# A 3x3 convolution with 2x2 max pooling: rows 33 to 63 of the first image pair in one casting load, the second pair's first 33 rows in another, and a new order

## Chip, cores and metric

The kernel runs on one core of one Trainium2 chip. The metric is the device time of one execution in microseconds (us). The engines are TensorE (PE, with its weight loads as PEld), VectorE (DVE), ScalarE (ACT), GpSimd (POOL) and SyncE (SP, which here only issues transfers). Each has its own instruction queue and works through it in order; semaphores hold an instruction back until what it needs is done.

## The reference

```python
x:      16 images, 64 channels, 64 x 64, float32
weight: 128 x 64 x 3 x 3, float32
conv[b, co] += weight[co, ci, kh, kw] * x_pad[b, ci, kh:kh+64, kw:kw+64]      # padding 1
output[b, c, i, j] = max(conv[b, c, 2i:2i+2, 2j:2j+2])                        # 16 x 128 x 32 x 32
```

## The kernel before

**Tiles.** Two images make a pair: the 64 channels of the first lie on partitions 0 to 63, those of the second on 64 to 127. There are 8 pairs, each in SBUF as one bf16 tile `xb[p]` of 66 rows (a zero row above and below). A pair is cut in four quarters of 16 image rows, which give 8 pooled rows; a quarter of one image (half `h` = 0 or 1) has 8 x 64 = 512 columns, one PSUM bank of `acc`. The 32 quarters are numbered `s` in the order of work; `PLACES` says which pair and quarter of it `s` is (0, 1, 3, 5 are the first pair, 2, 4, 6, 7 the second, 8, 9, 10, 11 and so on the next ones). The last quarter, 31, is done in two halves, 31 and 32.

**Arithmetic.** For a pooled row one needs the larger of two convolution rows, even and odd. What both have in common is added once, after the maximum. Quarters of type K form two accumulators from raw rows, `ta` = (G2-G1) x[2i+1] + G0 x[2i-1] and `tb` = (G0-G1) x[2i] + G2 x[2i+2], and add G1 (x[2i] + x[2i+1]) to the larger. Quarters of type W (27 of 32) use differences: e = x[2i] - x[2i+1], d = x[j+1] - x[j-1], s = x[2i] + x[2i+1]; `ta` = GM e + G0 d, `tb` = GM e + G2 d, and GP s is added to the larger of -`ta` and `tb`. GM and GP are half of G0 + G2 minus or plus G1. Every product is three matmuls, one for each column tap, on 64 partitions; those of the two halves run side by side on the two halves of PE's rows.

**Order.** The whole program is the text `ORDER`. Each word is one step, taken in this order and put on its engine's queue, so the text fixes every queue. A word is a name, the quarter and the half; `+` chooses the other engine (or way), `&` does two things in one instruction. The names that matter here:

- `g0a`, `g0b`, `g1`, `g2` cast weight blocks on ACT; `D0`, `D2a`, `D2b`, `GS`, `GM`, `GP` form their differences and sums on DVE (`GS` with `+`); `u..` copies a block's first slot behind its last (a ring copy); `T..` and `H..` transpose a block on PE; `V..` copies it out of PSUM.
- `L.p.lo.hi` is a load of rows lo to hi of pair p by POOL, cast from float32 to bf16 on the way (line 325). `XOa`, `XOb`, `XEa`, `XEb` and `X1` to `X4` are casts on ACT or DVE of rows that SP has loaded as float32 (lines 430 and 432).
- `F.k.part` are the products of quarter 0. `PA1`, `PA2`, `PB1`, `PB2`, `PR` are those of type K, `P2` (e), `P0` and `P3` (d), `P1` (s) those of type W. A product waits in a list until the other half has one too, then the six matmuls are issued in turn. The first product of an accumulator takes the next bank from `BANKS`, and PE then waits until whatever held that bank has been read.
- `D`, `E`, `S` form d, e, s (lines 319 and 304). For d the plain word is POOL and `+` is DVE; for e `+` is POOL; s is always on DVE. `Da` and `Db` are the two halves of a d.
- `SE` copies `ta` to a bank for `tb` after P2 (ACT, line 352); `EV` copies `ta` to SBUF (line 346, or 342 for type K); `MX` takes the maximum on DVE (line 380); `OD` copies the odd columns on ACT (line 390); `CM` takes the maximum over columns on DVE (line 409). With `OD+` there is no copy and `CM` reduces both columns itself (line 405). When both halves are done, the result is stored from SP (line 422).

An instruction on POOL is made to wait for the last SBUF operation on DVE that stands before it in `ORDER`:

```python
def on_vector(inst):
    sbuf_op[0] = inst
    return inst

def on_gpsimd(inst):
    behind(inst, sbuf_op[0])
    return inst
```

The first pair's rows 0 to 48 come as float32 through SP (`kfirst` in two parts, `ksecond`, `kthird`) and are cast on ACT and DVE; rows 49 to 63 and all other pairs come through POOL's casting loads.

Of the kernel before, what the change touches and what calls it, by code (L numbers as in the profile page):

```python
# [11 lines left out]
def kernel(  # L12
# [85 lines left out]
    kthird = const.tile([128, 2 * R, W], FP32)  # L98
    nc.sync.dma_start(out=kthird, in_=rows_of(0, FAR + 2 * R, FAR + 4 * R))
# [206 lines left out]
    def row_sum(s, alt, joint):  # L306
        combine("s", s_pool, ADD, s, joint, False)
# [145 lines left out]
    for m in PRODUCTS:  # L453
        steps[m] = lambda s, h, m=m: product(m, s, h)
    either = {
        "GS": outer_sum, "D": lambda s, alt: row_d(s, not alt, 0, 2 * span_of(s)[1]),
        "Da": lambda s, alt: row_d(s, alt, 0, R),
        "Db": lambda s, alt: row_d(s, alt, R, 2 * R),
         "SE": seed, "EV": evac, "OD": odd,
# [12 lines left out]
    for m in ("G1", "G2"):  # L472
# [14 lines left out]
        OD.0.1 P0.3.1 P3.3.1 PA2.5.0 EV.3.1 P0.3.0 MX.1.0 CM.0.1 PA1.5.1 PR.1.0 EV.3.0 D+.2 MX.3.1 E&.2
        PB1.5.0 PR.1.1 EV.5.0 OD.1.1 OD.1.0 S&.4 P1.3.1 P2.2.1 P3.3.0 CM.1.1 CM.1.0 D.4 OD.3.1 CM.3.1 SE.2.1
        PB2.5.0 MX.3.0 P2.4.0 PA2.5.1 P2.4.1 MX.5.0 EV.5.1 P0.2.1 E&.6 P1.3.0 P3.2.1 SE.4.0 SE.4.1 OD.3.0 D+.7
        CM.3.0 P0.4.1 PR.5.0 EV.2.1 OD.5.0 P0.4.0 EV.4.1 P2.6.0 D+.6 P3.4.1 MX.2.1 SE.6.0 E+.8 P2.6.1 MX.4.1  # L490
        P1.2.1 P3.4.0 P0.6.0 P3.6.0 CM.5.0 P1.4.1 EV.4.0 S&.6 SE.6.1 EV.6.0 S&.10 OD.2.1 CM.2.1 P0.6.1 PA1.9.0
        P2.7.0 EV.6.1 OD.4.1 PA2.9.0 P3.6.1 MX.4.0 D.10 P1.4.0 PB1.5.1 PB2.5.1 L.4.0.64 MX.6.1 P1.6.1 SE.7.0
        P2.8.1 EV.9.0 MX.6.0 MX.5.1 OD.4.0 PR.5.1 P0.7.0 EV.7.0 D+.8 CM.4.0 P1.6.0 OD.6.1 SE.8.1 CM.6.1 P0.8.1
        P2.7.1 P3.7.0 OD.6.0 CM.4.1 CM.6.0 OD.5.1 E&+.10 P2.8.0 SE.8.0 EV.8.1 P3.8.1 PB1.9.0 CM.5.1 P0.8.0
        P2.10.1 MX.7.0 SE.7.1 PB2.9.0 EV.8.0 P3.8.0 SE.10.1 S&.13 P0.7.1 EV.7.1 P1.7.0 Db.13 S&.9 MX.9.0
        PR.9.0 P2.2.0 P3.7.1 OD.7.0 MX&.8.1 P0.10.1 P3.10.1 P1.8.1 P1.8.0 D.11 CM.7.0 E&+.12 EV.10.1 MX.7.1
        SE.2.0 P1.7.1 MX.10.1 OD.9.0 CM.9.0 OD.8.0 CM.8.0 OD.8.1 CM.8.1 P1.10.1 P2.11.0 PA1.15.1 OD.7.1 CM.7.1
        SE.11.0 P0.2.0 P3.2.0 PB1.9.1 EV.2.0 OD.10.1 S&.14 PA2.15.1 P2.10.0 P0.11.0 MX.2.0 P1.2.0 PB2.9.1
        L.5.0.64 CM.10.1 SE.10.0 EV.15.1 PA1.9.1 E.19 OD.2.0 P0.10.0 EV.11.0 EV.10.0 P3.10.0 P2.11.1 PA2.9.1
        Da.13 S&.18 SE.11.1 E&.17 P3.11.0 CM.2.0 P2.12.1 PA1.15.0 EV.9.1 MX.10.0 P1.10.0 MX.11.0 MX.9.1  # L500
        P0.11.1 D.12 D+.16 SE.12.1 OD.10.0 CM.10.0 EV.11.1 PA2.15.0 P3.11.1 MX.11.1 E+.14 PR.9.1 P0.12.1
# [25 lines left out]
        E+.30 P1.27.1 OD+.27.1 Db+.28 P2.30.1 P1.27.0 EV.29.0 MX.29.0 SE.30.1 P2.28.0 P0.28.1 P3.28.1 CM.27.1
        OD.27.0 CM.27.0 D.30 P1.29.0 P2.30.0 S.30 EV.28.1 P0.30.1 MX.28.1 SE.28.0 OD.29.0 CM.29.0 EV.30.1 D.31
        E+.31 P2.29.1 P0.28.0 SE+.30.0 SE.29.1 P3.30.1 P3.28.0 P0.30.0 P1.28.1 EV.28.0 MX.30.1 P3.30.0 P0.29.1
        P2.31.1 MX.28.0 OD.28.1 CM.28.1 EV.30.0 MX.30.0 P3.29.1 SE.31.1 P1.28.0 P2.31.0 P1.30.0 P0.31.1 S.31  # L530
        EV.29.1 OD.28.0 SE.31.0 MX.29.1 P0.31.0 PA1.32.0 PA2.32.0 CM.28.0 EV.31.1 PB1.32.0 PRA.32.0 P1.30.1
# [68 lines left out]
```

## Time and profile before

| | us |
|---|---|
| three runs | 102.54, 102.1, 101.49 |
| median | 102.1 |
| profiled run | 101.6 |
| its span | 99.7 |
| first product on PE | 6.54 |
| end of the last matmul | 95.46 |
| last stores issued | 96.36 (SP), 96.56 (ACT) |

Times inside a run are counted from the start of the span. The granted clock is 1.00 in every stage up to the last matmul. Until about 28 us the DMA engines are busy all the time, with the casting loads from 7.5 on:

| load | issued | landed |
|---|---|---|
| weights, SP | 0.74 | 3.7 |
| `kfirst`, two parts | 1.17, 1.64 | 4.6, 5.9 |
| `ksecond` (512 KB of float32) | 2.11 | 7.6 |
| `kthird` (512 KB of float32) | 2.58 | 8.9 |
| L.0.49.64 (240 KB of bf16) | 6.28 | 10.9 |
| L.1.0.17 (272 KB) | 6.97 | 13.5 |
| L.1.17.33 (256 KB) | 7.50 | 14.7 |
| L.1.33.64 (496 KB) | 8.58 | 17.3 |
| L.2.0.33 (528 KB) | 9.10 | 20.1 |
| L.2.33.64 (496 KB) | 12.23 | 23.0 |
| L.3.0.64 (1024 KB) | 14.02 | 28.2 |

In the lines of the profile, "L193 PE" is line 193 of the kernel on PE; `out<-in` are the tiles; in lists by group the figures after the bar are busy time and the mean in ns of one instruction, then the idle time before them and what ended it; in a timeline the first two figures are start and duration, x the number of instructions merged, and the bracket the idle time before.

### The profile page before, as it was taken

The page shows a single profiled execution, that of the slowest core. Times are in us where ns is not written, and L with a number is a line of the kernel's source. Part 1 is how long each engine was busy: PE and PEld are TensorE (multiplying, and loading weights), DVE is VectorE, ACT ScalarE, POOL GpSimd, SP SyncE. Part 2 cuts the span into 40 slices and gives each one's busy share as a digit, 9 for nine tenths or more (in the row PEclk, how much of TensorE's full clock was granted, in tenths as well). Part 3 has the DMA queues.
Part 4 walks back from the last instruction along what each step waited for, and adds up shares of the span by engine and source line. Part 5 has one row for each costly group of instructions (what it writes and reads, how often), then busy time and mean ns, then how long its engine had stood idle before and what let it go on. Part 6 is the DMA issues. An engine that isn't in the chain of part 4 may idle for free.

```text
span 99.7 us, 2469 instructions
## 1 busy us (share of the span) xinstructions
PE 94.7 (95%) x887; PEld 58.2 (58%) x887; DVE 91.7 (92%) x196; ACT 84.5 (85%) x190; POOL 54.4 (55%) x45
## 2 busy tenths in 40 slices
PE   6999999999999999999999999999999999999920
PEld 2478445546647777855556566666665555556910
DVE  2498999999999999999999999999999999999960
ACT  5498797998899898999989999999999998999610
POOL 2047031733783951748397966963946499690000
PEclk9999999999999999999999999999999999999995
DMA  2999999999999889999079995999253060630363
GB/s 33 347 349 129 149 217 211 222 238 227 262 215 198 191 301 177 207 188 362 28 105 214 202 315 78 197 167 371 65 196 107 7 210 0 210 108 0 117 207 102
DMA packets 11036, 18.03 MB, mean 181 GB/s; under 512 B 784, under 2 KB 9104, under 8 KB 10384
## 3 DMA queue, kind: packets, MB, share of 16 engines
q0 software_dynamic: 1584, 7.59, 42.8%
q1 hardware_dynamic: 9296, 10.16, 30.0%
q8 instruction: 7, 0.11, 0.5%
q10 hardware_dynamic: 144, 0.13, 0.4%
q14 instruction: 5, 0.04, 0.1%
HBM read 17.07 MB, written 8.39 MB: 255 GB/s over the span
## 4 chain that ended last, share of the span: by engine, by line
PE 94%; DVE 1%; DVEq 0%; issue 0%
PE acc L193 89%; PE acc L544 4%; PE acc L145 2%; DVE o L398 1%; DVEq L595 0%
## 5 line engine op out<-in xcount | busy, mean ns | idle before, releaser
L193 PEld LDWEIGHTS <-wt 64*128 64x128 bf16 x858 | 55.5, 94 | 32.8 <-issue 3.8
L193 PE MATMUL acc<-d,wt 64*128 64x512 bf16 (+3 forms) x324 | 66.6, 373 | 0.0
L193 PE MATMUL acc<-s,wt 64*128 64x504 bf16 (+3 forms) x204 | 45.5, 367 | 0.0
L319 POOL TENSOR_TENSOR d<-xb 128x1024 bf16<-128x1024 bf16 (+1 forms) x18 | 33.3, 1860 | 18.3 <-DVE s L304 9.8
L380 DVE TENSOR_TENSOR acc<-acc,ev 128x512 f32<-128x512 f32 (+1 forms) x60 | 40.0, 685 | 1.1 <-PE acc L193 0.3
L193 PE MATMUL acc<-e,wt 64*128 64x512 bf16 (+2 forms) x162 | 40.1, 373 | 0.0
L346 ACT ACTIVATE ev<-acc 128x512 f32<-128x512 f32 (+1 forms) x54 | 31.9, 597 | 2.5 <-PE acc L193 2.0
L352 ACT COPY acc<-acc 128x512 f32<-128x512 f32 (+1 forms) x53 | 30.4, 576 | 3.0 <-PE acc L193 0.9
L193 PE MATMUL acc<-xb,wt 64*128 64x512 bf16 (+7 forms) x168 | 24.6, 327 | 0.0
L390 ACT COPY od<-acc 128x256 f32<-128x256 f32 (+1 forms) x54 | 19.0, 375 | 2.2 <-PE acc L193 1.8
L409 DVE TENSOR_TENSOR o<-acc,od 128x256 f32<-128x256 f32 (+1 forms) x54 | 20.7, 412 | 0.1
L304 POOL TENSOR_TENSOR e<-xb 128x512 bf16<-128x512 bf16 (+1 forms) x9 | 14.2, 1583 | 3.7 <-DVE d L319 3.7
L325 POOL DMA_DIRECT2D xb<-in_x_dram x11 | 6.2, 562 | 12.8 <-DVE wt L159 5.0
L304 DVE TENSOR_TENSOR s<-xb 128x1024 bf16<-128x1024 bf16 (+1 forms) x18 | 11.5, 646 | 0.2 <-ACT xb L430 0.2
L319 DVE TENSOR_TENSOR d<-xb 128x1024 bf16<-128x1024 bf16 (+1 forms) x12 | 7.8, 649 | 0.0
L405 DVE TENSOR_REDUCE o<-acc 128x256 f32<-128x512 f32 x10 | 6.8, 681 | 0.0
L342 ACT COPY ev<-acc 128x512 f32<-128x512 f32 x9 | 5.2, 592 | 0.7 <-PE acc L193 0.7
L304 DVE TENSOR_TENSOR e<-xb 128x1024 bf16<-128x1024 bf16 (+1 forms) x8 | 5.0, 619 | 0.0
L544 PE MATMUL acc<-const-bfloat16-1.0 128*128 128x512 bf16 x8 | 3.6, 626 | 0.8 <-PEq L581 0.8
L170 ACT CAST wq<-wraw 128x192 bf16<-128x192 f32 (+2 forms) x4 | 1.7, 444 | 1.7 <-DMA wraw<-in_weight_dram 1.7
L145 PEld LDWEIGHTS <-wq 128*128 128x128 bf16 x21 | 1.7, 117 | 1.7 <-DVE wq L443 0.9
L443 DVE TENSOR_TENSOR wq<-wraw 128x192 bf16<-128x192 f32 x1 | 0.5, 499 | 2.2 <-DMA wraw<-in_weight_dram 2.2
(27 smaller groups left out, 21.6 us busy)
## 6 DMA issues: line engine op xcount, KB each, us to landing
out_dram<-o SPq DMA_DIRECT2D x31, 256.0 KB, 4.3
xb<-in_x_dram POOLq DMA_DIRECT2D x5, 1024.0 KB, 9.6
xb<-in_x_dram POOLq DMA_DIRECT2D x2, 496.0 KB, 9.7
xb<-in_x_dram POOLq DMA_DIRECT2D x1, 528.0 KB, 11.0
ksecond<-in_x_dram SPq DMA_DIRECT2D x1, 512.0 KB, 5.5
kthird<-in_x_dram SPq DMA_DIRECT2D x1, 512.0 KB, 6.3
wraw<-in_weight_dram SPq DMA_DIRECT2D x1, 288.0 KB, 3.0
kfirst<-in_x_dram SPq DMA_DIRECT2D x1, 288.0 KB, 3.5
```

Source lines behind the costliest of these rows:

```text
L193: nc.tensor.matmul(acc[:, t, i0:i1, o0:o1], wt[lo : lo + CI, tap_of(m0, kw, h), :], rows(lo, i0, i1, c0, c1), start=start and kw == 1, sto ...
L304: note(engine.tensor_tensor(out=dst, in0=in0, in1=in1, op=op))
L319: engine.tensor_tensor(out=diffs[s][:, lo:hi, :], in0=t[:, f + 1 + lo : f + 1 + hi, :], in1=t[:, f - 1 + lo : f - 1 + hi, :], op=SUB)
L325: inst = on_gpsimd(nc.gpsimd.dma_start(out=xb[p][:, lo + 1 : hi + 1, :], in_=rows_of(p, lo, hi)))
L342: (nc.vector.tensor_copy if alt else nc.scalar.copy)(out=dst, in_=src)
L346: nc.scalar.mul(dst, src, -1.0)
L352: (nc.vector.tensor_copy if alt else nc.scalar.copy)(out=acc[:, t, i0:i1], in_=acc[:, ta[s, h], i0:i1])
L380: nc.vector.tensor_tensor(out=t, in0=t, in1=ev[s][:, h, i0:i1], op=MAX)
L390: nc.scalar.copy(out=dst, in_=acc[:, tb[s, h], i0:i1, 1::2])
L405: nc.vector.tensor_reduce(out=o[:, h, i0:i1], in_=t.rearrange("p r (w two) -> p r w two", two=2), axis=mybir.AxisListType.X, op=MAX)
L409: nc.vector.tensor_tensor(out=o[:, h, i0:i1], in0=t[:, :, 0::2], in1=od[s][:, h, i0:i1], op=MAX)
L544: nc.tensor.matmul(acc[:, n].rearrange("p a b -> p (a b)"), ones[:, 0:128], ones, start=True, stop=True, skip_group_check=True)
```

## The change

1. `kthird` and its transfer go, with the casts `X3` and `X4` (both on ACT). The casting load of rows 49 to 63 becomes one of rows 33 to 63. Quarter 3 (rows 32 to 47) now gets its rows from it.
2. L.1.0.17 and L.1.17.33 become L.1.0.33. L.2.33.64 comes ahead of L.2.0.33, L.7 ahead of L.6.
3. `GM` and `GP` may run on either engine (`outer`), and `GP` runs on POOL. s may run on POOL: it does so for five words of `ORDER` (quarter 15 alone, and in one instruction for the pairs of quarters at 21, 23, 24 and 31).
4. The results of quarters 12, 16 and 20 are stored in two transfers, one for each image, instead of one.
5. `ORDER` and `BANKS` are new from the first word to the last. PE has the same instructions, 858 product matmuls and 21 transposes among them. 17 transposes stand before the first product (20 before), and four, TGP, HGM and HGP, behind PA1 of quarter 1. Among the choices of engine: VG0 and VG2 go from DVE to ACT, XEa from ACT to DVE, X1 from DVE to ACT; 13 d of full size are on DVE (10 before); 12 odd copies are left out (10 before).

```diff
     ksecond = const.tile([128, 2 * R, W], FP32)
     nc.sync.dma_start(out=ksecond, in_=rows_of(0, FAR, FAR + 2 * R))
-    kthird = const.tile([128, 2 * R, W], FP32)
-    nc.sync.dma_start(out=kthird, in_=rows_of(0, FAR + 2 * R, FAR + 4 * R))
...
+    def outer(m, op, alt):
+        engine, note = (nc.gpsimd, on_gpsimd) if alt else (nc.vector, on_vector)
+        note(engine.tensor_tensor(out=slots(m), in0=gsum, in1=g1, op=op))
...
     def row_sum(s, alt, joint):
-        combine("s", s_pool, ADD, s, joint, False)
+        combine("s", s_pool, ADD, s, joint, alt)
...
+    SINGLY = (12, 16, 20)
...
-        if s < N - 1:
+        if s < N - 1 and s not in SINGLY:
             dst = out[2 * p : 2 * p + 2, :, q * R : (q + 1) * R, :].rearrange("b c h w -> c b (h w)")
             queue.dma_start(out=dst, in_=o.rearrange("p b h w -> p b (h w)"))
         else:
-            dst = out[2 * p + h, :, q * R : (q + 1) * R, :].rearrange("c h w -> c (h w)")
-            queue.dma_start(out=dst, in_=o[:, h].rearrange("p h w -> p (h w)"))
+            for k in (0, 1) if s < N - 1 else (h,):
+                dst = out[2 * p + k, :, q * R : (q + 1) * R, :].rearrange("c h w -> c (h w)")
+                queue.dma_start(out=dst, in_=o[:, k].rearrange("p h w -> p (h w)"))
...
-        "X3": lambda alt: cast_next(kthird, FAR + 2 * R, 0, alt),
-        "X4": lambda alt: cast_next(kthird, FAR + 2 * R, 1, alt),
...
     ORDER = """
-        D0 TD0 g1 D2a TG1 TD2 g2 TG2 uG1+ uD2+ HG1 GS+ D2b HD2 GM uG2+ uD0+ HG2 GP HD0 g0a VD2 L.0.49.64 TGM
-        VD0 L.1.0.17 uGM+ TG0 HGM VG1 TGP uG0+ g0b HG0 VG0+ L.1.17.33 XOa+ VG2+ XEa+ uGP F.0.0 XOb+ XEb+ S.0
-        VGM F.2.0 F.1.0 X1+ F.0.1 F.1.1 EV.0.0 F.2.1 F.3.0 F.3.1 PA1.1.0 X2 PB1.1.0 L.1.33.64 PA1.1.1 PB1.1.1
-        L.2.0.33 HGP PA2.1.1 X4 PB2.1.1 X3 VGP+ EV+.0.1 MX.0.0 PR.0.0 OD.0.0 PA2.1.0 MX.0.1 S.1 EV.1.1 E.3
...
+        g1 g0b uG1+ D0 TD0 D2a TG1 D2b GS+ L.0.33.64 uD0+ uD2+ HD0 TD2 HD2 g0a g2 TG0 uG0+ uG2+ VD2 TG2 GM XEa
+        HG0 XOa+ HG2 VG0 HG1 TGM F.0.0 VD0 F.2.0 XOb+ F.1.1 F.1.0 F.0.1 L.1.0.33 XEb+ F.2.1 VG2 F.3.0 F.3.1 X1
+        PA1.1.1 PA1.1.0 EV+.0.1 VG1 L.1.33.64 GP+ L.2.33.64 uGP EV.0.0 S.0 MX.0.1 uGM+ TGP X2 HGM HGP S.1
+        PB1.1.0 PR.0.1 PA2.1.0 OD.0.1 MX.0.0 PR.0.0 PB2.1.0 PA2.1.1 PB1.1.1 VGM Db.3 E.3 EV.1.0 OD.0.0 P2.3.1
+        S&.3 CM.0.1 P2.3.0 PB2.1.1 CM.0.0 PA1.5.1 VGP+ EV.1.1 Da+.3 PA1.5.0 SE.3.1 MX.1.0 PR.1.0 SE.3.0 P0.3.1
+        PA2.5.0 MX.1.1 PR.1.1 P0.3.0 EV.3.1 OD.1.0 L.2.0.33 D+.2 E&.4 P3.3.1 EV.5.0 S&.4 EV.3.0 P2.2.1 OD.1.1
+        CM.1.0 P3.3.0 SE.2.1 PA2.5.1 PB1.5.0 PB2.5.0 MX.3.1 MX.3.0 P1.3.1 P1.3.0 EV.5.1 OD.3.1 P2.4.1 CM.1.1
+        MX.5.0 P2.4.0 CM.3.1 L.3.0.64 D.4 E&.7 P0.2.1 OD.3.0 CM.3.0 SE.4.1 SE.4.0 PR.5.0 P3.2.1 P3.4.1 P0.4.1
...
+        EV.25.0 P0.26.0 CM.23.1 MX.25.0 SE.26.1 EV.26.0 CM.24.0 D.27 E+.30 E+.28 P3.26.0 P1.25.0 P2.27.1
+        MX.26.0 OD.25.1 SE.27.1 P2.27.0 P0.26.1 P3.26.1 P1.26.0 CM.25.1 E.29 P2.29.0 P0.27.1 D+.29 EV.26.1
+        OD.25.0 CM.25.0 P3.27.1 MX.26.1 SE.27.0 P2.28.1 P0.27.0 P3.27.0 P1.26.1 EV.27.1 MX.27.1 OD.26.0
+        CM.26.0 SE.29.0 EV.27.0 MX.27.0 SE.28.1 P1.27.1 P0.29.0 OD+.27.1 P3.29.0 P2.30.1 CM.27.1 EV.29.0
+        MX.29.0 OD.26.1 D.28 P0.28.1 D.30 E+.31 S&+.31 SE.30.1 P1.27.0 EV.28.1 P3.28.1 P2.28.0 CM.26.1
+        OD+.27.0 D.31 SE.28.0 CM.27.0 P0.30.1 P1.29.0 P2.29.1 P2.30.0 OD.29.0 EV.30.1 MX.28.1 P0.28.0 CM.29.0
...
```

More of the change, by code (lines that the diff above doesn't have):

```diff
@@ L455 @@
     either = {
-        "GS": outer_sum, "D": lambda s, alt: row_d(s, not alt, 0, 2 * span_of(s)[1]),
+        "GS": outer_sum, "GM": lambda alt: outer(GM, SUB, alt), "GP": lambda alt: outer(GP, ADD, alt),
+        "D": lambda s, alt: row_d(s, not alt, 0, 2 * span_of(s)[1]),
         "Da": lambda s, alt: row_d(s, alt, 0, R),
         "Db": lambda s, alt: row_d(s, alt, R, 2 * R),
-         "SE": seed, "EV": evac, "OD": odd,
+        "SE": seed, "EV": evac, "OD": odd,
         "XOa": lambda alt: cast_first(1, MID, alt),
@@ L487 @@
[L487 to L501, printed above, removed]
@@ L527 @@
[L527 to L531, printed above, removed]
@@ new lines @@
+        D+.6 OD.5.0 CM.5.0 D+.7 EV.2.1 MX.2.1 P2.6.1 P2.6.0 P1.2.1 P0.4.0 SE.6.0 P3.4.0 EV.4.0 SE.6.1 P0.6.1
+        P0.6.0 P3.6.0 EV.4.1 EV.6.0 S&.6 PA1.9.0 S&.10 MX.4.0 P1.4.0 P3.6.1 PA2.9.0 EV.6.1 PB1.5.1 MX.4.1
+        MX&.6.1 OD.2.1 CM.2.1 OD.4.0 P1.4.1 OD.4.1 PB2.5.1 P2.7.0 CM.4.0 P1.6.0 EV.9.0 E+.8 P1.6.1 SE.7.0
+        P2.8.0 OD.6.0 OD.6.1 P0.7.0 P3.7.0 P2.8.1 E&+.11 CM.4.1 MX.5.1 SE.8.1 PB1.9.0 PR.5.1 L.4.0.64 D+.8
+        EV.7.0 CM&.6.0 SE.8.0 P0.8.1 S&.12 OD.5.1 EV.8.1 P2.7.1 P3.8.1 P0.8.0 SE.7.1 PB2.9.0 S&.8 CM.5.1
@@ L538 @@
-        "461357260154362075310672415306217301536"
+        "0123456723047165037245130672453604312075630423146753046523106247530273140653267130564702163752640713"
+        "267543065412765310472360415273016271523"
     )
@@ L557 @@
         elif name == "CM":
-            (colmax_both if joint else colmax)(*args[: 2 - joint], free=len(closing) - closing.index(i) if i in closing else 0)
+            free = len(closing) - closing.index(i) if i in closing else 0
+            (colmax_both if joint else colmax)(*args[: 2 - joint], free=free)
         elif name in joined:
```

66 lines of the change are left out of this document (34 added, 32 removed).

## The prediction

> **What bounds it.** First the page's busy times, then the chain of waits, in order of time.
>
> ```profile
> PE 94.7 (95%) x887; PEld 58.2 (58%) x887; DVE 91.7 (92%) x196; ACT 84.5 (85%) x190; POOL 54.4 (55%) x45
> ```
>
> ```profile
> 0.78 3.57 PE acc L544 x8
> 4.35 2.17 PE acc L145 x20
> 6.54 4.05 PE acc L193 x60
> ...
> 10.76 84.27 PE acc L193 x780
> ...
> 95.04 1.29 DVE o L398 x2
> ```
>
> PE carries 94% of the chain. Around the span of 99.7 lie 1.9 us (profiled run 101.6); the median of the three runs, 102.1, is 0.5 above that, so I sum against 101.6 and add 0.5. PE's own work is fixed: in the timeline matmuls of 504 or 512 columns start 0.216 apart per pair. From the groups by form, 738 such x 0.108 = 79.7, 96 of 252/256 columns (0.109 per pair) 5.3, 24 others 1.6: 86.6. From the first product (6.54) to the last matmul's end (95.46), less its 0.27 run-out, are 88.6. So about 2.0 us of waiting can be won there at most; the change leaves the 858 matmuls as they are. The timeline of weight loads shows where the waits are (loads follow each other by some 0.11, so idle less 0.11 is the wait):
>
> ```profile
> 10.52 0.10 PEld L145 LDWEIGHTS <-wq 128*128 128x128 bf16 x1 [0.42 <-issue]
> ...
> 18.77 2.49 PEld L193 LDWEIGHTS <-wt 64*128 64x128 bf16 x25 [0.40 <-issue]
> 21.58 0.33 PEld L193 LDWEIGHTS <-wt 64*128 64x128 bf16 x5 [0.32 <-issue]
> ...
> 28.31 0.52 PEld L193 LDWEIGHTS <-wt 64*128 64x128 bf16 x6 [0.24 <-issue]
> ...
> 44.06 1.84 PEld L193 LDWEIGHTS <-wt 64*128 64x128 bf16 x19 [0.35 <-DVE o L409]
> ```
>
> Waits are small and many. Those I followed end on DVE or ACT: at 18.77, P1 of quarter 3 starts 0.05 after the row max that DVE ran from 18.02 to 18.71. In the stages 14:30, 30:60 and 60:88 DVE is busy 15.99, 29.84 and 27.64 us, so it is the second limit everywhere.
>
> **Costs by form.** Rows used below (mean ns of one before the last bar):
>
> ```profile
> L319 POOL TENSOR_TENSOR d<-xb 128x1024 bf16<-128x1024 bf16 x13 | 27.6, 2128 | 15.7 <-DVE s L304 9.8 <-PE acc L193 5.2 <-DVE e L304 0.7
> L304 DVE TENSOR_TENSOR s<-xb 128x1024 bf16<-128x1024 bf16 x14 | 9.8, 711 | 0.0
> L430 ACT CAST xb<-kthird 128x512 bf16<-128x512 f32 x2 | 1.1, 621 | 0.0
> ```
>
> DVE: four joint sums (0.71) and one of a quarter (0.42) go to POOL, -3.26; three differences come, +2.08; e +0.42 -0.69; GP -0.50; copies VG0 and VG2 go to ACT, -0.71; X1 goes (-0.44), XEa comes (+0.3, from 0.44 for 512 elements); two more direct reductions, 2 x (0.68-0.42) = +0.53. Sum -2.3 of 91.7. ACT: X3, X4 -1.24, X1 +0.62, XEa -0.45, two copies +0.94, two odd copies -0.76: -0.9. POOL: sums 4 x 2.12 + 1.16, d -6.6, e +1.2, GP in float32 without a row (0.35 for the 64-element copy to 1.16 for 512; I take 0.6): +4.8, of 45 us free. These totals cost nothing unless a wait ends there, so I walk the stages.
>
> **Start.** ACT reaches the first image cast after two 192-casts (0.44 apart), a 128- and a 64-cast and six ring copies (0.146 apart): 6.09. Now it has five, and no longer waits for GM: 2 x 0.44 + 0.32 + 0.21 + 5 x 0.146 from 3.74 = 5.88. First product at 6.33 instead of 6.54. But four transposes now stand after PA1 where there was one (10.52), 3 x 0.07 later: the 0.2 goes back. G0's copy on ACT (0.47 after 6.2) and the next cast hold F.2.0 and F.1.1 for 0.05 to 0.1 each, and PR of half 1 waits for DVE's chain evacuation, G1 copy, sum, max (0.61 + 0.27 + 0.33 + 0.69 from 8.15): 10.05. Before, PR.0.0 began at 10.69 with 0.54 more product work behind it; now 10.1, so 0.05 ahead. Sum 0 (bounds -0.2 and +0.2).
>
> **Loads.** 512 KB of float32 leave SP's queue (349 GB/s in the page's slices: 1.5 us). The casting load grows from 240 to 496 KB; two of 272 and 256 KB become one of 528.
>
> ```profile
> xb<-in_x_dram POOLq DMA_DIRECT2D x2, 496.0 KB, 9.7
> ...
> xb<-in_x_dram POOLq DMA_DIRECT2D x1, 272.0 KB, 6.5
> ...
> xb<-in_x_dram POOLq DMA_DIRECT2D x1, 240.0 KB, 4.6
> ```
>
> In 9:12.5 the casting queue moved 0.46 MB in 248 packets at 102% of the engines, 132 GB/s; in 15:20, with rows of 31 and 33, 1.01 MB at 100%, 202 GB/s. Larger rows are cheaper, so the small ones at 132 become large at 202. The merged load is issued 0.31 behind gsum (as now behind GP: 5.97, 6.28), at 5.45. With SP done at 7.35 it lands near 9.8; the same data had landed by 10.88 before. Needed: Db and E of quarter 3 on DVE (0.33 + 0.42) before P2.3 at 12.07, so by 11.25. Covered by 1.4 (0.4 at the later bound): nothing. Second-pair rows 0 to 33 come by 12.5 instead of 14.74, before D.2 at 14.15. Only L.2.0.33 is later, behind Da.3 on POOL: issued at 14.1 instead of 9.1, landed some 20, wanted at 23.3. Moved past in POOL's queue, it holds up none.
>
> **10 to 30 us.** P0.3 (13.52, 0.12 lost) finds its seed copied at 13.92, wants it at 14.0: -0.07. DVE then runs d, e, s (0.60 apart), o (0.33), max, max from 14.15: the second max ends at 17.57, P1.3.0 wants it at 17.75, so the 0.28 wait of 18.77 goes. What is late next: P2.6.0 now takes the bank that CM.3.0 frees; behind max, o, e, o DVE ends that at 19.95, PE comes at 19.69: +0.26. P1.2.1 waits for MX.2.1, end 22.07, and starts 0.1 earlier than now. At 28 SE.8.1 and MX.5.1 bind again, some 0.2 of the 0.3. Sum -0.2 (bounds -0.5 and 0).
>
> **30 to 88.** Waits here add up to 0.47 (44.06 to 76.16). I did not follow each; with DVE 2.3 and ACT 0.9 lighter, bounds -0.47 and 0, I take -0.2. DVE stays 98% busy, so not all goes.
>
> **End.** The POOL chain d 28, d 30, e 31, s 31, d 31 (2.13 + 2.13 + 1.16 + 2.12 + 1.16 = 8.7) follows DVE's d 29 (end near 82.05): d 30 at 86.35 where P0.30.1 wants 86.4, d 31 at 90.9 where P0.31.1 wants 90.75: +0.15. P3.31.0 comes 0.3 earlier and frees the 0.1 wait of P1.31.0: -0.1. The split stores of quarters 12, 16, 20 are three more SP issues of 0.4 in a queue that waits 67 us for DVE: 0. Tail after the last matmul unchanged.
>
> Sum 0 - 0.2 - 0.2 + 0.05 = -0.35: 101.2 against 101.6; against the median 101.7.
>
> **A rule against the change.** POOL and DVE hinder each other:
>
> ```profile
> 52.88 1.15 POOL L304 TENSOR_TENSOR e<-xb 128x512 bf16<-128x512 bf16 x1
> ...
> 53.59 1.00 DVE L304 TENSOR_TENSOR s<-xb 128x1024 bf16<-128x1024 bf16 x1
> ```
>
> A 0.69 us sum that begins under a POOL operation took 1.00 and ended 0.56 after it. The order makes POOL wait for DVE ("behind"), not the reverse. The Trainium skill, page "SBUF — State Buffer", section "Who interferes with whom", says that a DVE instruction with two SBUF inputs and a GpSimd instruction that reads SBUF share a read port, and that the later one waits for the whole of the first. By that rule the trace agrees, 1.00 against 0.69; the sum above takes in none of it, and what it would make of the time is rival 4.
>
> **Rivals** (on the median's scale).
> 1. Larger gain: the lighter DVE removes the waits of 30 to 88 (0.47), half of the 0.56 lost after 88, and 0.4 of those before 30: -1.3, 100.8. For: every wait followed ends on DVE or ACT. Against: CM.3.0 shows how the next one fills in.
> 2. No gain: DVE's order only moves its deadlines: 102.1.
> 3. Slower, the merged load lands late. Point: 11.25. Nearest row: 4.6 us for 240 KB, plus 256 KB at 132 GB/s (2.0): 12.05, +0.8; the 496 KB rows, which queued behind others, took 9.7: 15.15, +3.9. I take +1.5, nearer the first: 103.2. For: half the quarter's data now waits for one semaphore. Against: fewer bytes in front than now. The Trainium skill, the same page, section "SBUF: two separate sides", says that a DVE float32 copy in SBUF can keep GpSimd from writing a DMA's descriptors. No run here shows it; by that rule XEa would hold this load for at most X2's 0.44 us, within the 1.4 of cover.
> 4. Port: s 23 and e 21 run on POOL back to back (4.2 us behind d 20); DVE's d 21 comes some 0.5 behind their end. If POOL is 0.5 to 1.5 late, DVE stands for up to 1.0: 102.7.
> That the change is not made is excluded: the instruction order shows one casting load and no third float32 load.
>
> **Numbers.** Forecast 101.7 (own range 101.1 to 102.3): 0.45; larger gain 0.21; no gain 0.11; late load 0.11; port 0.12. One per cent, about what a measurement of this kernel can tell from no change, is 101.1 and 103.1. Faster: 0.19 of the larger gain and 0.07 of the forecast, 0.26. Slower: 0.08 of the late load, 0.05 each of port and of the cost of stages not followed, 0.18. Same 0.56. Range from the larger gain, less 0.3 if no wait is left before 30, to the late load: 100.5 to 103.2.
>
> **What will show it.** Merged load landed before 11.25 and P2.3 near 12.1; no idle at P1.3.0, but one of 0.2 to 0.3 at P2.6.0; DVE near 89.4 busy; s on POOL at 2.1 with no DVE instruction over 1 us beside it; d 31 about 0.1 before or after PE wants it. Wrong if a wait above 0.5 appears before 15 or after 82, or if DVE's busy time doesn't fall.

## The result: 1.3% slower, and the profile after

| | before | after |
|---|---|---|
| median, us | 101.92 (101.49 to 102.54, 4 runs) | 103.28 (102.95 to 104.51, 4 runs) |
| ratio | | 1.0128, 95% interval 1.0082 to 1.0175 |
| profiled run / its span | 101.6 / 99.7 | 103.17 / 101.3 |
| first product on PE | 6.54 | 6.55 |
| end of the last matmul | 95.46 | 96.34 |
| from there to the end of the span | 4.28 | 4.96 |

(Before, a fourth run of 101.74 has joined the three.) The change makes the kernel slower; the median lies just above the range of 100.5 to 103.2. A ratio leaves out executions that lie more than 1.5% above the fastest of their kernel (three of twelve in b3, d2 and e1 below, four in e2), so for a kernel that scatters it reads lower than the medians over all, which are the times given.

The granted clock is 1.00 in the stages shown here, as before. The page's busy times:

```profile
PE 94.6 (93%) x887; PEld 61.2 (60%) x887; DVE 90.2 (89%) x191; ACT 83.5 (82%) x188; POOL 58.9 (58%) x47
```

By these totals nothing is wrong: DVE lost 1.5, ACT 1.0, PE does the same. The chain of waits (start, duration, what) shows more. Before, PE's products were one piece from 10.76 to the tail; now the chain leaves PE twice:

```profile
6.62 3.30 PE acc L195 x54
9.92 0.33 PE acc L143 x4
10.25 4.77 PE acc L195 x42
...
19.26 0.75 DVE e L306
20.01 0.35 DVE o L412
20.36 0.04 issue
20.40 15.46 PE acc L195 x140
...
38.34 1.27 DVE e L306
39.61 0.03 issue
39.64 0.41 DVE s L306
40.06 0.60 DVE d L321
40.66 0.34 DVE o L412
41.00 0.04 issue
41.04 54.80 PE acc L195 x519
95.84 0.02 issue
95.86 1.29 DVE o L401 x2
```

The e of 1.27 us stands out (the whole instruction took 1.38): one of the same size (one quarter) takes 0.42 elsewhere. The weight loads show what PE lost (idle time in brackets; 0.11 of it is the usual distance, the rest a wait):

```profile
18.07 1.82 PEld L195 LDWEIGHTS <-wt 64*128 64x128 bf16 x18 [0.22 <-issue]
20.41 1.17 PEld L195 LDWEIGHTS <-wt 64*128 64x128 bf16 x12 [0.52 <-ACT acc L354]
...
41.05 1.41 PEld L195 LDWEIGHTS <-wt 64*128 64x128 bf16 x15 [1.12 <-issue]
```

The wait of 1.0 at 41 is new and larger than any of before. Compared at equal amounts of product work (columns of the matmuls started), PE is level with the kernel before after 5 us of work, 0.2 behind after 7, 0.1 behind at 38 us, 1.0 to 1.1 from 41 to 44, 0.96 at 65 and 0.89 at the end. So of the 1.57 us between the two profiled runs 1.0 appears in one place, 0.68 comes after the last matmul, and the rest nearly cancels. Windows of the two traces (stretch, length, then busy us of PE, PEld, DVE, ACT, POOL) confirm it; before:

```profile
40.00:42.00 2.00, 2.00 (x22) 1.60 (x19) 2.00 (x4) 1.87 (x5) 1.75 (x1) 1.00 1.02 205
42.00:82.00 40.00, 40.00 (x370) 24.06 (x367) 39.68 (x75) 37.98 (x83) 27.93 (x18) 1.00 0.69 177
```

and after:

```profile
40.00:42.00 2.00, 1.36 (x13) 0.56 (x11) 2.00 (x6) 0.79 (x3) 1.20 (x1) 1.00 0.85 239
42.00:82.00 40.00, 40.00 (x371) 27.78 (x369) 38.86 (x75) 37.86 (x83) 30.74 (x19) 1.00 0.64 173
```

Between 42 and 82 DVE has 0.8 us less to do and PE does one matmul more: a lighter DVE bought at most 0.1 where PE was full already.

**What happens at 38.** POOL and DVE, from their timelines:

```profile
37.77 1.67 POOL L306 TENSOR_TENSOR e<-xb 128x512 bf16<-128x512 bf16 x1 [1.92 <-PE acc L195]
```

```profile
37.73 1.99 DVE L306 TENSOR_TENSOR e<-xb 128x1024 bf16<-128x1024 bf16 x2
39.64 0.41 DVE L306 TENSOR_TENSOR s<-xb 128x512 bf16<-128x512 bf16 x1
39.98 0.68 DVE L321 TENSOR_TENSOR d<-xb 128x1024 bf16<-128x1024 bf16 x1
40.58 0.41 DVE L412 TENSOR_TENSOR o<-acc,od 128x256 f32<-128x256 f32 x1
```

POOL's e is that of quarter 19, which the new order gives to POOL (`E+.19`; before, `E.19` on DVE). The bracket names a matmul, but the product that it stands for was long done. The e also needs pair 4, and the load L.4, issued at 26.94, landed at 37.63. DVE's joint e of quarters 16 and 17 needs the same load. So in this trace one landing released both engines within 0.04 us (DVE had been free for 0.07 us). DVE's e came first, POOL's took 1.67 instead of the 1.16 of that size, and DVE's next e (quarter 14) began at 38.34 and ended at 39.72, 0.28 after POOL's: 1.38 instead of 0.42. The reduction at 40.58 (CM.10.1) frees the bank that PE wants at 40.04; it came 0.96 late, and PE stood for 1.0. The Trainium skill, page "SBUF — State Buffer", section "Who interferes with whom", says that a DVE instruction with two SBUF inputs and a GpSimd one that reads SBUF exclude each other for the whole of the one that starts first. By that rule the trace agrees: each of the two waited for the other's end.

That both waited for the load is not what makes the collision. In ten traces with this e on POOL it starts 0.13 to 0.14 after L.4's landing, and DVE loses 0.96. In seven of the ten (a0, a3, b1, b4, d4, e1 and e2 below) DVE was still busy with d of quarter 13 when L.4 landed, so POOL's e came first, and it was DVE's joint e that took 1.64 instead of 0.68. POOL and then DVE in a0 (the two e of DVE are merged):

```profile
37.77 1.54 POOL L306 TENSOR_TENSOR e<-xb 128x512 bf16<-128x512 bf16 x1 [1.28 <-DMA xb<-in_x_dram]
```

```profile
38.22 1.98 DVE L306 TENSOR_TENSOR e<-xb 128x1024 bf16<-128x1024 bf16 x2
```

**The merged load.** Its landing was forecast for 9.8 and needed by 11.25. In this trace it was issued at 5.35 and landed at 11.42, and DVE's half d of quarter 3 waited 0.26 for it, which just cost nothing on PE. In another execution of the same kernel (e1 below) it landed at 12.43:

```profile
11.45 0.42 DVE L321 TENSOR_TENSOR d<-xb 128x512 bf16<-128x512 bf16 x1 [0.26 <-DMA xb<-in_x_dram]
```

```profile
12.45 0.42 DVE L321 TENSOR_TENSOR d<-xb 128x512 bf16<-128x512 bf16 x1 [1.39 <-DMA xb<-in_x_dram]
```

So the first trace was a lucky one, and its reading alone would have missed this wait.

### The profile page after: what moved, and what is told of

It is laid out like the page before. It is cut to its first block, busy times and chain, and to the rows that moved or that the text cites. A ratio compares the mean times of both kernels' runs of the same rounds, so it can differ in the third digit from the quotient of the medians.

```text
span 101.3 us, 2451 instructions
## 1 busy us (share of the span) xinstructions
PE 94.6 (93%) x887; PEld 61.2 (60%) x887; DVE 90.2 (89%) x191; ACT 83.5 (82%) x188; POOL 58.9 (58%) x47
## 4 chain that ended last, share of the span: by engine, by line
PE 79%; DVE 9%; ACT 3%; DMA 3%; issue 1%; DVEq 0%
PE acc L195 77%; DMA wraw<-in_weight_dram 3%; DVE e L306 2%; DVE acc L382 2%; DVE o L412 2%; ACT wq L168 1%; PE acc L143 1%; DVE o L401 1%; DVE d L321 1%; DVE o L408 1%; ACT ev L348 1%; ACT ev L344 0%; ACT wq L132 0%; DVE s L306 0%; ACT od L393 0%
## 5 line engine op out<-in xcount | busy, mean ns | idle before, releaser
L195 PEld LDWEIGHTS <-wt 64*128 64x128 bf16 x858 | 58.4, 94 | 30.6 <-issue 3.8
L195 PE MATMUL acc<-d,wt 64*128 64x512 bf16 (+3 forms) x324 | 65.2, 373 | 0.0
L195 PE MATMUL acc<-s,wt 64*128 64x504 bf16 (+3 forms) x204 | 46.7, 367 | 0.0
L321 POOL TENSOR_TENSOR d<-xb 128x1024 bf16<-128x1024 bf16 (+1 forms) x14 | 26.8, 1920 | 9.3 <-DVE s L306 5.0
L195 PE MATMUL acc<-xb,wt 64*128 64x512 bf16 (+6 forms) x168 | 24.6, 327 | 0.6 <-DVE o L412 0.6
L306 POOL TENSOR_TENSOR e<-xb 128x512 bf16<-128x512 bf16 (+1 forms) x10 | 15.8, 1593 | 8.2 <-DVE s L306 4.3
L327 POOL DMA_DIRECT2D xb<-in_x_dram x10 | 5.6, 564 | 11.8 <-DVE s L306 4.9
L306 POOL TENSOR_TENSOR s<-xb 128x1024 bf16<-128x1024 bf16 (+1 forms) x5 | 9.6, 1926 | 2.9 <-DVE s L306 2.2
L321 DVE TENSOR_TENSOR d<-xb 128x1024 bf16<-128x1024 bf16 (+1 forms) x15 | 9.7, 645 | 0.3 <-DMA xb<-in_x_dram 0.3
L408 DVE TENSOR_REDUCE o<-acc 128x256 f32<-128x512 f32 x12 | 8.2, 682 | 0.0
L306 DVE TENSOR_TENSOR s<-xb 128x1024 bf16<-128x1024 bf16 (+1 forms) x13 | 7.8, 620 | 0.0
```

Source lines behind the costliest of these rows:

```text
L195: nc.tensor.matmul(acc[:, t, i0:i1, o0:o1], wt[lo : lo + CI, tap_of(m0, kw, h), :], rows(lo, i0, i1, c0, c1), start=start and kw == 1, sto ...
L306: note(engine.tensor_tensor(out=dst, in0=in0, in1=in1, op=op))
L321: engine.tensor_tensor(out=diffs[s][:, lo:hi, :], in0=t[:, f + 1 + lo : f + 1 + hi, :], in1=t[:, f - 1 + lo : f - 1 + hi, :], op=SUB)
L327: inst = on_gpsimd(nc.gpsimd.dma_start(out=xb[p][:, lo + 1 : hi + 1, :], in_=rows_of(p, lo, hi)))
L408: nc.vector.tensor_reduce(out=o[:, h, i0:i1], in_=t.rearrange("p r (w two) -> p r w two", two=2), axis=mybir.AxisListType.X, op=MAX)
```

## The experiments

Three theories stood: the landing of L.4 starts a collision of POOL and DVE (1), DVE's order alone is to blame (2), or the time went elsewhere (3). Waits in the table are those of PE in the profiled execution of each kernel, taken as the idle time of its weight loads less 0.11; "end" is from the last matmul to the end of the span. Edits of `ORDER` show only the words around the place.

| run | first-pair load landed | wait at 13 | wait at 41 | last matmul | end | time | ratio to before (95%) |
|---|---|---|---|---|---|---|---|
| a0 | 12.07 | 0.9 | 0.8 | 96.81 | 5.02 | 103.43 | 1.0171 (1.0135 to 1.0207) |
| a1 | 12.09 | 0.9 | 0, but 0.6 at 56.5 | 97.05 | 4.98 | 103.91 | 1.0212 (1.0176 to 1.0247) |
| a2 | 12.40 | 1.4 | 1.3 | 97.62 | 5.16 | 104.56 | 1.0262 (1.0219 to 1.0305) |
| a3 | 12.02 | 1.0 | 0.8 at 42.1, 0.3 at 47.3 | 97.07 | 5.02 | 103.83 | 1.0207 (1.0174 to 1.0240) |
| b1 | 12.13 | 0.7 | 0.8 | 96.88 | 4.97 | 103.20 | 1.0147 (1.0098 to 1.0196) |
| b2 | 9.79 and 10.93 | 0 | 0.3 | 95.51 | 4.98 | 103.36 | 1.0167 (1.0115 to 1.0220) |
| b3 | 12.69 | 1.6 | 0 | 96.60 | 5.03 | 102.85 | 1.0069 (1.0027 to 1.0112) |
| b4 | 11.86 | 0.8 | 0.8 | 96.60 | 4.73 | 102.78 | 1.0111 (1.0064 to 1.0159) |
| c1 | 10.68 and 11.81 | 0 | 0 | 95.66 | 4.69 | 102.16 | 1.0008 (0.9969 to 1.0046) |
| c2 | 9.78 and 10.98 | 0 | 0 | 95.23 | 4.63 | 102.03 | 1.0000 (0.9967 to 1.0033) |
| c3 | 11.76 | 0.4 | 0 | 96.04 | 4.31 | 101.99 | 0.9999 (0.9970 to 1.0028) |
| c4 | 11.19 (rows 49 to 63) | 0 | 0 | 95.36 | 4.99 | 102.45 | 1.0055 (1.0017 to 1.0092) |
| d1 | 10.47 and 11.61 | 0 | 0 | 95.49 | 4.25 | 101.64 | 0.9980 (0.9946 to 1.0014) |
| d2 | 12.29 | 1.1 | 0.9 | 97.10 | 4.19 | 101.78 | 0.9973 (0.9938 to 1.0007) |
| d3 | 10.66 and 11.81 | 0 | 0 | 95.14 | 4.29 | 101.44 | 0.9964 (0.9933 to 0.9994) |
| d4 | 10.66 | 0 | 0.85 | 100.14 | 5.02 | 106.87 | 1.0477 (1.0427 to 1.0527) |
| e1 | 12.43 | 1.15 | 0.8 | 97.16 | 5.01 | 103.12 | 1.0096 (1.0056 to 1.0137) |
| e2 | 10.62 | 0 | 0.85 | 96.27 | 4.19 | 102.22 | 1.0008 (0.9972 to 1.0045) |

The kernel before ran beside each letter: 101.55 (a, b), 101.91 (c), 101.75 (d) and 101.64 (e).

**a0**, the changed kernel itself.

> The changed kernel once more, the measure for the others. All theories: 103.3, ratio to the kernel before 1.008 to 1.018, a PE wait of 1.0 us near 41 in its trace, with a DVE e of one quarter that takes 1.4 instead of 0.42 near 38. If the 0.68 us that its end (last matmul to end of span) took more than that of the kernel before belongs to the kernel, it is 4.9 to 5.0 again; if it is chance of one run, it lies somewhere between 4.2 and 5.0.

It confirmed the loss and the end of 5.0, and showed the wait at 13 that the first trace had not. The wait near 41 was 0.8, and the e of one quarter took its usual 0.41: here the joint e before it was the one that stood under POOL's.

**a1**, e of quarter 19 later:

```diff
- P2.10.0 E+.19 MX.2.0
+ P2.10.0 MX.2.0
- L.6.0.64 E+.18 D.18
+ L.6.0.64 E+.18 E+.19 D.18
```

> The POOL difference e of quarter 19 is moved behind that of quarter 18, so nothing on POOL waits for L.4 and nothing on POOL runs beside DVE's two e at 37.7. Theory 1 (collision): the e of quarter 14 takes 0.42, DVE is 0.9 earlier, the PE wait near 41 is below 0.15, time 0.9 to 1.0 shorter: 102.3, ratio 1.003. Theory 2 (order on DVE): five difference and sum instructions ahead of CM.10.1 hold up PE by themselves; 0.4 to 0.5 of the wait stays, 102.8. Theory 3 (the time went elsewhere: sums on POOL, the closing steps): as the changed kernel, 103.2 to 103.3.

As theory 1 has it, DVE's two e take 1.02 together instead of 1.99 and the wait at 41 is gone with DVE's order unchanged, which ends theory 2. The time did not fall, though. The extra 1.1 us on POOL pushes d of quarter 18 against DVE's d of quarter 20; DVE in this trace:

```profile
38.24 1.02 DVE L306 TENSOR_TENSOR e<-xb 128x1024 bf16<-128x1024 bf16 x2
...
54.39 1.75 DVE L321 TENSOR_TENSOR d<-xb 128x1024 bf16<-128x1024 bf16 x1
```

and POOL:

```profile
53.47 2.12 POOL L321 TENSOR_TENSOR d<-xb 128x1024 bf16<-128x1024 bf16 x1
```

DVE's d, 0.68 elsewhere, began under POOL's and ended 0.55 after it. The collision was moved, not removed, and PE paid for it at 56.5 (0.6) and 57.5 (0.3).

**a2**, the load L.5 behind e 19:

```diff
- P2.10.1 MX.7.0 L.5.0.64 P0.7.1 D+.10
+ P2.10.1 MX.7.0 P0.7.1 D+.10
- P2.10.0 E+.19 MX.2.0
+ P2.10.0 E+.19 L.5.0.64 MX.2.0
```

> The load L.5 is issued behind the e of quarter 19 (near 37) instead of at 30.3, as in the kernel before. Theory 1a (L.4 is late because L.5 shares the DMA engines with it): L.4, issued at 26.9, lands at 36.3 to 36.7 instead of 37.63; e 19 on POOL ends by 37.8 and costs DVE 0.3 at its d of quarter 13 instead of 0.96; PE waits 0.3 near 41; 102.6, ratio 1.006. Theory 1b (L.4 is late by itself, or because of the stores): it lands within 0.3 of 37.6, the collision and the 1.0 stay, 103.2. L.5 lands near 47 and is wanted at 48.8: no wait in either.

1a fell: L.4, issued at 27.91, landed at 38.93, 11.0 after its issue, against 10.7 (first trace) and 10.1 (a0) with L.5 beside it. L.5 is not what makes it late.

**a3**, ` CM.10.1` ahead of S.14 and D+.16 on DVE.

> On DVE, CM.10.1 goes ahead of s 14 and d 16, so the bank that PE waits for near 41 is free 0.94 earlier, while the collision and its 0.96 on DVE stay. Theory 1: the single wait of 1.0 goes, but DVE (98% busy) is still 0.96 late, and the wait comes back in pieces at the next row maxima up to 47; 102.8 to 103.2. Theory 2 (only the order mattered): it stays gone, 102.3.

As theory 1 says: PE's wait comes back in two pieces, 0.8 at 42.1 and 0.3 at 47.3.

**b1**, the merged load ahead: ` D0 L.0.33.64 TD0` instead of ` GS+ L.0.33.64`.

> The merged load of rows 33 to 63 is issued behind the first weight difference D0 (near 4.2) instead of behind the weight sum (5.3). Theory A (the merged load lands after 11.25, at 12.0 to 12.4 in the four runs above, and P2.3 waits for it): it lands near 11.0 to 11.2, the PE wait at 12.9 falls from 0.85 to under 0.2, 102.6 to 102.8, 0.6 to 0.8 below the changed kernel. Theory B (the DMA engines are the limit, an earlier issue only lengthens the transfer or holds up kfirst and ksecond): it lands at 11.8 or later, or the first product starts later than 6.5; no gain, 103.4.

Theory B: issued at 4.42, 0.94 earlier than in a0, it landed at 12.13 against 12.07. Its first packets ended at 6.5 to 7.0 instead of 7.5 to 8.0, and the rest ran so much slower.

**b2**, the merged load as two:

```diff
- GS+ L.0.33.64 uD0+
+ GS+ L.0.33.49 L.0.49.64 uD0+
```

> The merged load as two, rows 33 to 48 first, then 49 to 63, both behind the weight sum. Theory A: rows 33 to 48 land near 10.3 (4.6 us for 240 KB in the kernel before, plus issue), P2.3 does not wait, 0.8 gained there; the loads behind it come some 0.6 later, so L.1.0.33 (14.7 in the second run of the changed kernel) lands at 15.2 and DVE's d of quarter 2, then wanted at 14.2, waits for it: 0.5 to 0.9 of the 0.8 goes back; 102.6 to 103.4. Theory B: as the changed kernel or worse, 103.4 to 104.

The trace did what theory A says: rows 33 to 48 landed at 9.79, P2.3 did not wait, and even the second half landed at 10.93, 1.1 before the whole in a0. The times did not follow (103.36; the profiled execution was the fastest of its six, 102.36). What the others waited for no trace shows.

**b3**, L.4 early:

```diff
- D.4 E&.7
+ D.4 L.4.0.64 E&.7
- PR.5.1 L.4.0.64 D+.8
+ PR.5.1 D+.8
```

> L.4 is put behind POOL's d of quarter 4 (issued near 20) instead of behind e 11 (27 to 27.6). Theory 1 (collision of POOL's e 19, started by the landing of L.4, with DVE's e): L.4 follows L.3 and lands by 36; e 19 runs right behind POOL's d 11 (about 36 to 37.5), before DVE's e at 38; no DVE instruction of s, d, e between 36 and 42 takes over 0.8; the PE wait near 41 is below 0.2; 102.6, 0.65 to 0.85 below the changed kernel. Theory 2 (order on DVE): 0.4 of the wait stays, 103.0. If L.4 still lands at 37 or later the run decides nothing.

L.4 landed at 33.89 and theory 1 held: POOL's e 19 runs right behind d 11 and before DVE's e. POOL and then DVE:

```profile
37.07 1.15 POOL L306 TENSOR_TENSOR e<-xb 128x512 bf16<-128x512 bf16 x1
```

```profile
38.84 1.02 DVE L306 TENSOR_TENSOR e<-xb 128x1024 bf16<-128x1024 bf16 x2
```

Both have their own durations again and there is no wait at 41. The merged load was later than ever (12.69) and cost 1.6. The 12 times lie between 101.67 and 103.71, which is what a kernel looks like whose loads sometimes come in time.

**b4**, no divided stores: `SINGLY = ()`.

> The results of quarters 12, 16 and 20 are stored in one transfer each again, three SP issues less. From the last matmul's end to the end of the span it was 4.28 in the kernel before and 4.95 in the changed kernel, though both do the same there. Theory C1 (these 0.67 us depend on how many instructions SP and POOL have had, such as on where the next block of instructions must be fetched): it becomes 4.2 to 4.4, and 102.8. Theory C2 (not on the stores): 4.9 to 5.0 and 103.4, the same as the changed kernel.

The gap on SP went, but half of it came back in other waits of the closing steps: 4.73, between C1 and C2. It took d1 and d2 to see why.

**c1**, b2, b3 and b4 together.

> The changed kernel with three edits together: rows 33 to 63 of the first pair as two loads, L.4 behind d 4, no divided stores of quarters 12, 16, 20. Theory (late merged load + collision started by L.4's landing + closing steps are the whole of the loss): no PE wait over 0.25 near 12.9 and near 41, last matmul ends at 95.2 to 95.4, closing steps 4.2 to 4.4 (SP's and POOL's part of it 0.06 and 0.2 again), 101.3 to 101.6, ratio to the kernel before 0.996 to 1.001. Rival (the new order itself is slower, sums on POOL): 102 or more with the waits gone.

Both load waits are gone and the last matmul is 0.2 behind the kernel before instead of 0.9 to 1.4 (a0, after). By the ratio (1.0008) the kernel is level with the kernel before: these three are the loss, to within the 0.4% of the interval. The rival, an order that stays slower with the waits gone, is out to the same extent, though the forecast time of 101.3 to 101.6 was missed (102.16 beside 101.91), and so was the end (4.69 for 4.2 to 4.4). New at 24.7 is a wait of 0.5 for L.2.0.33 (landed 23.23).

**c2**, and `OD.3.0 CM.3.0 E&.7` instead of `E&.7 P0.2.1 OD.3.0 CM.3.0`.

> As the last, and on DVE CM.3.0 goes ahead of e 7, so that the bank P2.6.0 waits for near 20 (0.40 in every run of the changed kernel) is free 0.6 earlier and e 7 no longer runs beside POOL's d 4 (0.83 for 0.69). Theory: that wait goes below 0.1 and the 0.4 stays won: 100.9 to 101.2, ratio 0.993 to 0.997. Rival: e 7 or d 6 is then late for P2.7 or P2.6 and the wait moves: as the last.

The rival: 0.42 stays at 20.3. The e of quarters 6 and 7 is one instruction, and P2.6.0 needs it as much as the bank.

**c3**, the first part of the change alone on the kernel before (`kthird`, X3, X4 out, `L.0.33.64` for `L.0.49.64`).

> The kernel before with the first part of the change alone: no third float32 load, no X3 and X4, L.0.33.64 in the place of L.0.49.64. Theory (a casting load of 496 KB takes 6.3 to 7.4 us there): issued near 6.0 to 6.3 it lands at 12.3 to 13.2, DVE's e of quarter 3, at 10.91 now, waits 1.3 to 2.2 for it, P2.3 comes 0.5 to 1.3 later; 102.2 to 102.9. Rival (fewer bytes on the DMA engines let it land by 11): 101.5, as the kernel before.

The load took 5.6 us and landed at 11.76, earlier than expected; PE waits 0.4 at 12.3, and the last matmul is 0.58 later than before. By the times (101.75 to 102.22 against 101.29 to 103.61) no difference can be told: inconclusive.

**c4**, the divided stores alone on the kernel before.

> The kernel before with the results of quarters 12, 16 and 20 stored in two transfers each. Theory C1 (the closing steps depend on the number of SP's instructions, 0.48 more with three stores more): SP's last drain comes 0.5 after its last wait instead of 0.06, the end of the span 0.3 to 0.5 later; 101.9 to 102.0. Rival (the closing steps depend on something else in the changed kernel): 101.55, no difference.

C1: with last matmul at 95.36 as before, the end takes 4.99 instead of 4.28, 0.5% of time. A gap of 0.42 accounts for more than half of the 0.71; the rest stays open.

**d1** and **d2**, three idle memsets on POOL, on c2 and (with `SINGLY = ()`) on the changed kernel:

```diff
+    spare = const.tile([128, 3], FP32)
+        "N": lambda k: nc.gpsimd.memset(spare[:, k : k + 1], 0.0),
- L.7.0.64 SE.13.1
+ L.7.0.64 N.0 N.1 N.2 SE.13.1
```

> As c2_and_cm30_first, with three memsets of one element on POOL (near 48, POOL idles there) that nothing reads, so that POOL has 77 records as in the kernel before and the 68th comes before the closing steps. Theory C1 (in every trace so far a gap of 0.42 stands before POOL's record number 68 and SP's number 79, counted from 0, wherever they fall; it costs only when it falls in the closing steps): no gap over 0.2 among POOL's closing records, last matmul to end of span 4.2 to 4.3 instead of 4.6, 0.4 less than c2: 101.3 to 101.6 where the kernel before is at 101.6 to 101.9, ratio 0.995 to 0.998. Rival C2 (the gap belongs to the closing steps, not to the count): it stays, as c2.

> The changed kernel with both closing gaps moved: no divided stores (SP) and the three memsets (POOL); the late merged load and the collision stay. Theory C1: last matmul to end 4.2 to 4.4 instead of 5.0, ratio to the kernel before 1.008 to 1.011 instead of 1.0171, so the closing steps are 0.6 to 0.8 us of the loss. Rival C2: 4.7 as without the divided stores alone, ratio 1.011 to 1.013.

C1 both times. Adding three instructions that do nothing takes the end from 4.63 to 4.25 in d1. In d2 it takes 4.19 where a0 took 5.02. The time of d2 fell by more than forecast (0.9973 for 1.008 to 1.011), and its executions spread from 100.84 to 103.44. Its trace is of the second slowest of the twelve (103.06).

**d3**, and ` MX.2.1 D+.7` for `D+.7 EV.2.1 MX.2.1`.

> As d1, and on DVE the row max of quarter 2, half 1, goes ahead of d 7 (P1.2.1 waits 0.18 for it near 22.4). Theory: DVE's order there has room, d 7 is wanted only near 25.5: the 0.18 goes and 0.1 to 0.2 stays won: 101.2 to 101.5. Rival: DVE is the limit to the next wait at 28, nothing is won, as d1.

The 0.18 at 22.4 went, but 0.25 came at 23.0. With 101.44 (101.20 to 101.91 in 12 runs) this version is 0.4% below the kernel before (interval 0.1% to 0.7%) and the steadiest of all built on the change. It is the best of the 18 runs here, so its lead may in part be chance, and its trace does not show where it comes from: its last matmul ends 0.32 before that of the kernel before, but its products had begun 0.42 earlier (6.12 against 6.54). Its page, and the last matmuls of its chain in one piece:

```profile
PE 93.9 (94%) x887; PEld 60.6 (61%) x887; DVE 89.3 (90%) x191; ACT 83.4 (84%) x188; POOL 59.1 (59%) x51
```

```profile
20.18 74.45 PE acc L196 x699
```

**d4**, the five sums on DVE again (`S&+` to `S&`, `S+.15` to `S.15`).

> The changed kernel with its five sums s of quarter 15 and of the pairs at 21, 23, 24 and 31 on DVE again. It also has five POOL records less, so the 68th does not come at all: 0.43 of closing time goes by theory C1. Theory S1 (the sums on POOL are a gain, since DVE is 98% busy): DVE 3.3 us heavier, waits of 1 us or more after 48, last matmul 0.5 to 2 us later, 103.5 to 104.5. Theory S2 (the sums on POOL are the loss, through port and late d): last matmul earlier than 96.3, 102.5 or less.

S1, and beyond its upper bound: 106.87, with DVE at 94.1. (POOL's record 68 did come, as its last, and the end is 5.02.) Waits of 0.3 to 1.0 follow from 48 on, and three of its sums take 1.0 to 1.2 beside POOL's d. The sums on POOL are what this order lives on.

**e1** and **e2**, the changed kernel and d2 side by side.

> The changed kernel once more, beside the next kernel on one chip, because d2 gave 0.9973 in a session where the changed kernel was not run. If the sessions are alike: ratio 1.013 to 1.018, last matmul to end of span 5.0. If the waits for loads come and go with the session: ratio as low as 1.005.

> d2 again (no divided stores, three memsets on POOL). Theory: the closing steps alone are worth 0.6 to 0.9 us: ratio 0.006 to 0.009 below the run beside it, last matmul to end 4.2. Rival (the memsets or the undivided stores act on something before the closing steps as well): 0.012 or more below it.

103.12 against 102.22: the closing steps are worth 0.9 us by time, 0.82 by trace. The ratio of e1, 1.0096, lies between its two forecasts; the medians of all its executions stand at 1.015.

**What the loss is made of.** The closing steps, 0.7 to 0.9, in every trace with the divided stores and without the memsets; the collision at 38, 0.8 to 1.3 in every trace with this order there in which L.4 landed after 37 (0.3 in b2, where it landed at 36.1); and the merged load, 0 to 1.6 by the execution, where 10.62 (e2) costs nothing, 12.43 (e1) 1.15 and 12.69 (b3) 1.6. Against this stands a gain of at most some 0.3 by the times of d3. How often each load is late in executions that were not profiled stays open: d1 and d2 differ by 0.14 in time, though the trace of d2 has 2.0 us of waits that d1 has not. An estimate from that trace fits the spread: without its two waits the last matmul would end at 95.1 and the span would take 99.3, and the fastest execution of d2 (100.84) has a span of 99.1. So its faster executions probably lack both waits; no trace shows one.

## Why the prediction was wrong

- **Start**, 0 ± 0.2: right. In the 17 traces with the new order products begin at 6.12 to 6.55, 6.35 in their middle (forecast 6.33), and the four transposes behind PA1 give 0.2 back: after 7 us of work PE is 0.2 behind in the first trace and 0.1 ahead in a0.
- **Loads**, 0, "covered by 1.4": wrong, and the first step to fail. I took the 202 GB/s of 15:20 for the merged load since its rows are long. In the traces with this load issued at 5.2 to 5.4 its packets begin at 6.6 to 6.9 and move at 125 to 147 GB/s up to 10.0 (105 to 124 of 128 packets of 3968 bytes); the last ones come up to 2 us later, and it lands at 10.6 to 12.7, not 9.8. So the rate was mis-sized, and the late last packets had no term. The other estimate, 4.6 us for 240 KB plus 256 KB at 132 GB/s, gave 12.05 and stood in rival 3 with a chance of 0.11; a0 has 12.07. Its price of 0.8 was right too (0.9). The row nearest to the place (9:12.5, the same queue behind the same SP loads) should have been taken. L.1.0.33 landed at 13.9 to 15.4 instead of 12.5; in no trace did DVE wait for it.
- **L.2.0.33**, landing near 20: 22.2 to 23.5. It was wanted at 23.3, so the slack hid most of the error (0.2 to 0.6 lost in b2, c1, d1, d4 and e2, where PE came earlier).
- **10 to 30**, -0.2: about half was won (0.2 behind at its beginning, 0.1 at its end). The wait at P1.3.0 went from 0.28 to 0.11, the new one at P2.6.0 is 0.41 instead of 0.26, and it hangs on e 6 and 7 (behind POOL's d 4, 0.83 for 0.68), not only on CM.3.0.
- **30 to 88**, -0.2, "I did not follow each", bounded above by 0: wrong, the largest error. A lighter total cannot bound a stage whose new order brings a new meeting of POOL and DVE. The mechanism was rival 4, at the right price (up to 1.0) and the wrong place: s 23 and e 21 did no harm (DVE's d 21 took 0.68), e 19 did, and DVE stood for 0.96. I had looked for POOL instructions that come late through POOL's own queue, not for one released by a load.
- **End**, +0.05: small as forecast, but of the other sign. From 82 on PE lost 0.1 less than before (1.0 behind at 82, 0.89 at the end).
- **Tail**, unchanged: wrong, 0.68. Three SP issues "in a queue that waits 67 us for DVE" cost nothing there, but they, and POOL's smaller number of records in the trace (73 against 77), moved a gap into the closing steps.
- **Engine totals**: right. DVE 90.2 less the 1.1 for which it stood under POOL (0.96 at 38, 0.15 at 19.2) is 89.1, forecast 89.4; ACT 83.5 against 83.6, POOL 58.9 against 59.2. Sums on POOL take 2.12 and no DVE instruction beside them takes over 1 us. That shows how little totals say.
- **Rivals and signs**: the terms of rival 1 (0.47, 0.28 and 0.4) add up to 1.15, not 1.3, and the 0.44 of rival 3 is X1's, not X2's; neither changes the outcome. The sign "a wait above 0.5 before 15" came in nine of the twelve traces with the whole load (not in the first); no sign was named for a wait of PE between 15 and 82, where the collision came.

## What to carry to other kernels

When an order is changed, list for every instruction on POOL what can release it. One that waits for a load starts at a time that the queue order doesn't set, and falls on whatever DVE does then: here DVE lost the same 0.96 whether or not it waited for the load too. Cost a new load by the slowest nearby row of the same stage, not by its row size, and give a landing within 1 us of its need the whole price. And look at the steps after the last result with the trace: instructions added anywhere may move a stall into them.

## What the runs showed that was not expected

**A gap at a fixed count.** Count the records of a queue in the trace from 0. Wherever it can be seen, some 0.42 passes idle ahead of POOL's record 68 and ahead of SP's record 79, whatever they are:

```
            POOL records 67, 68 start   SP records 78, 79 start   end after last matmul
after       100.17, 100.60              99.43, 99.88              4.96
c4          (in the work)               98.93, 99.38              4.99
c2          98.72, 99.15                (last one)                4.63
d4          104.62, 105.06              103.41, 103.85            5.02
d1          (in the work)               (last one)                4.25
```

In c4 SP has four records more than the kernel before and so meets the gap among the waits for the last stores; in the kernel before, as in c2 and d1, record 79 stands where SP waits for POOL anyway. The numbers count from the start: POOL has 69 records in d4, 73 in the changed kernel and 74 in c2, and the gap stays at 68.

The Trainium skill, page "Runtime: NRT & Kernel Launch", section "Instruction fetch mechanics", says that instructions are streamed in blocks and that crossing a block's boundary is mostly hidden. A fixed count would fit a boundary, but 0.42 is not hidden here, and in c2 no instruction transfer is recorded inside the gap (the nearest begin at 94.6 and 100.1). So the cause is argued, not shown; that the gap goes by the count is shown.

**One load of 496 KB is mostly later than two of 256 and 240 KB.** Issued at the same time behind the same loads, both halves had landed by 10.9 to 11.8 in five traces (the first by 9.8 to 10.7), the whole by 10.6 to 12.7 in eleven, 12.07 in their middle (b1, issued earlier, not counted). The traces differ in other edits too, and the two ranges overlap. In a0, 105 of its 128 packets (3968 bytes) had ended by 10.0; the last 11 ended between 10.5 and 11.7, while packets of the next load already ran beside them. Why they came last stays open.
